# An encoder layer on one core: another split of the first transfers, and four steps moved in a hand-ordered program

## The chip, the cores and the metric

The kernel runs on one core of a Trainium2 chip. The metric is the time of one execution on the device in microseconds (us), lower is better; the figure for the kernel before is the median of three runs. The core has a matrix engine (TensorE, PE in the profile, with its weight loads as a row PEld), three engines for elementwise work (VectorE = DVE, ScalarE = ACT, GpSimd = POOL) and queues that issue transfers between device memory and the on-chip buffers (SP above all, and ACT's own queue at the start; a q behind the engine's name in the trace is its queue's issue).

## The reference

One layer of an encoder is applied to a prompt of 256 tokens and to a sample of 2048 tokens, both of width 1024, with the same weights, in float32:

```python
h = rms_norm(x, g_pre)
q, k, v, z_a, u_f, z_f = split(h @ w_in)          # six groups of 512 columns
y_a = neighbourhood_attention(q, k, v, rpb)       # 8 heads, grid 64 wide, window 8 rows x 16 columns
y_f = fft2(u_f in groups of 64, over tokens and group).real @ w_fourier + b_fourier
mixed = concat([rms_norm(y_a, g_na) * silu(z_a), rms_norm(y_f, g_f) * silu(z_f)])
out = x + rms_norm(mixed @ w_out, g_post)
```

## The kernel before

**Products.** All data are float32. Each operand x is held as a high part xh (x cast to the matrix engine's type) and a low part xl = x - xh, so that a product of two operands is three matmuls into one sum, in the order of `mm3` (lines 163 to 166): high by high (L164), high by the weight's low part (L165), low by the weight's high part (L166); in these calls the first operand is the tokens, the second the weights. A row of the trace names both: L165 reads xh and a weight's low part (vl, or wc), L166 reads xl and a weight's high part. The cast is mostly done by ACT, the subtraction by DVE.

**Order.** The program is ordered by hand: each engine and each queue runs its instructions in the order in which the source issues them, and waits where an operand isn't there yet. Nothing is reordered by a scheduler.

**Stages**, with their places in the profiled execution:

- 0 to 118 us: v and u projections of the first six token tiles (128 tokens each), `p_mm`, and the prompt's z, k and q. Weights arrive in chunks of 128 x 512 (262 KB), are scaled by g_pre and split by `split_w` (ACT L261 writes the high part, DVE L262 the low part, both tiles called wc); token tiles are split by `x_split` (ACT L289, DVE L290).
- 118 to 158 us: `vu(0, ...)`, v and u of two more token tiles by a scheme of seven products of sums (as Strassen's). It has 14 steps of 12 matmuls, one step taking 2.72 us; the steps go j = 0 to 6, twice each. At chosen steps i a table of hooks runs other work ahead of the step's matmuls.
- 158 to 549 us: sixteen passes over pairs of weight blocks, with a second `vu` among them.
- 550 to 593 us: the Fourier stage, that is `z_mm`, `z_turn`, `z_32`, `pq`, then the product with the Fourier matrix.
- 593 to 862 us: attention; 862 to 952 us: output projection; then the last token tile's norm and stores.

**The first transfers (L624 to L627, L639).** x0[0] is one tile of 128 x 776 that holds the eight scales (g_pre, columns 0 to 7), and the first 256 features (two k-slices) of token tiles 0 (columns 8 to 263), 1 (264 to 519) and 2 (520 to 775). ACT's queue issues columns 0 to 519 as one transfer and then tile 2; SP's queue issues the first chunk of v weights (tile rv), then the second, then the rest. While they are on their way PE runs 10 matmuls on ones (L231, tile idle; in the trace each is two passes). Then, per pair of k-slices: first weight chunk, `x_split` of tile 0, copy of the scales to gpre (first pair only, DVE L639), `x_split` of tile 1, second weight chunk, tile 2.

**The hooks of vu(0).** `n_first(j)` makes the operand of product j: a cast of 128 x 2048 on ACT (L434, tile xh) and a subtraction on DVE (L435, tile xl), in full before the step's matmuls are issued. `op_load(j)` (L469) loads the weight sums of product j as two transfers vl, `op_split(j)` splits them (ACT L483 and DVE L484; L479 and L480 for j = 5, which also changes the sign). `rows_load` and `rows_square` load 1 MB of rows (L295, tile xm) and square them on ACT (L300). The finished products are added by DVE (L511, tiles uc, vuo, u4) and stored by SP (L354, vN and uN). `rows_load(6)` and the loads of j = 4 stand on SP's queue behind a store of v.

```python
for x, i in zip(range(3, 7), (0, 3, 5, 7)):
    at(i, n_first, x)
for x in range(4):
    at(2 * x + 1, rows_load, x + 5)
    at(2 * x + 4, rows_square, x + 5)
```

**The Fourier stage.** `z_mm(g)` multiplies into two PSUM tiles ptb (L1028), the same two for each g, and copies them out to zt (L1031, DVE and ACT); `z_turn(g)` transposes zt (L1038), with splits by ACT L1004 and DVE L1005; `z_32` handles the remaining 32 rows (L1019, L1009 to L1012); `pq(m)` is a product of the cosine table with the Fourier weights (L1081), whose result ACT copies to nq (L1087) and splits (ACT L1089, DVE L1090).

```python
z_mm(1); z_turn(0); z_32(0, 1); pq(1)
z_mm(2); z_turn(1); z_mm(3); z_turn(2); z_32(2, 3); z_turn(3); pq(0)
```

**The end.** `last_tile` computes the last output columns in two pieces, of 384 and 128, closes the norm, and for each half of 512 columns runs `residual`: a DVE instruction (L1758) and a store on SP (L1763).

Of the kernel before, what the change touches and what calls it, by code (L numbers as in the profile page):

```python
# [20 lines left out]
KC = 8  # L21
# [141 lines left out]
def mm3(nc, out, lh, ll, rh, rl, first, last):  # L163
    nc.tensor.matmul(out, lh, rh, start=first, stop=False)  # L164
    nc.tensor.matmul(out, lh, rl, start=False, stop=False)  # L165
    nc.tensor.matmul(out, ll, rh, start=False, stop=last)  # L166


def build(tc, A, O):
    nc = tc.nc  # L170
    es = ExitStack()
# [55 lines left out]
    nc.gpsimd.memset(onesq, 1.0)  # L227

    idle = ps.tile([128, 512], F32, tag="c", name="idle", bufs=1)
    for x in range(10):  # L230
        nc.tensor.matmul(idle[:, :128], onesq, onesq, start=True, stop=True)  # L231

    def gt(shape, dtype, name):
# [9 lines left out]
    W = {"v": [], "u": []}  # L243
# [12 lines left out]
    def split_w(m, src, ks=range(2)):  # L256
        for k in ks:
            h, l = chunk(), chunk()
            x = len(W[m])
            g = x0[0][:, x:x + 1] if m == "v" and x < 2 else gpre[:, x:x + 1]  # L260
            nc.scalar.activation(h, src[:, k], AF.Copy, scale=g)  # L261
            nc.vector.scalar_tensor_tensor(out=l, in0=src[:, k], scalar=g, in1=h.bitcast(F32),  # L262
                                           op0=ALU.mult, op1=ALU.subtract)
            W[m].append((h, l))
# [16 lines left out]
    def xload(c):  # L281
        xs[c] = load(BS, A["xs"][c - 3], "xr")

    def x_split(c, ks=slice(0, 8)):
        if c not in xh:
            xh[c] = gt(BS, F32R, "xh"), gt(BS, F32R, "xl")
        h, l = xh[c][0][:, ks], xh[c][1][:, ks]
        src = x_first(c, ks.start // 2) if c < 3 else xs[c][:, ks]
        nc.scalar.copy(h, src)  # L289
        nc.vector.tensor_tensor(out=l, in0=src, in1=h.bitcast(F32), op=ALU.subtract)  # L290


# [37 lines left out]
    def p_mm(m, c, kps, kks=None):  # L330
        if (m, c) not in acc:
            acc[m, c] = ps.tile([128, 512], F32, tag="b", name="mm", bufs=2) if (m, c) == ("u", 2) else mmt(512)
        xh_, xl_ = xh[c]
        for kk in kks or range(2 * kps[0], 2 * kps[-1] + 2):
            mm3(nc, acc[m, c], xh_[:, kk], xl_[:, kk], W[m][kk][0], W[m][kk][1], kk == 0, kk == KC - 1)

    def vu_out(m, c):
        s, b = PL[c]
# [110 lines left out]
    RV, RU = [], []  # L449
# [171 lines left out]
    def x_first(c, kp):  # L621
        return x0[kp][:, 8 * (kp == 0):][:, :768].rearrange("p (c k t) -> p c k t", c=3, t=128)[:, c]

    nc.sync.dma_start(RV[0][:, 0], A["wv"][0][:, 0])  # L624
    nc.scalar.dma_start(x0[0][:, :520], A["x0"])
    nc.scalar.dma_start(x0[0][:, 520:], A["x2"])
    nc.sync.dma_start(RV[0][:, 1], A["wv"][0][:, 1])  # L627
    nc.scalar.preload_act_table_set("natural_log_exp_and_others")
# [1 line left out]
    for kp in range(4):  # L630
        ks = slice(2 * kp, 2 * kp + 2)
        v = part(RV[kp // 2], kp)
        if kp:
            nc.sync.dma_start(v, part(A["wv"][kp // 2], kp))
            nc.sync.dma_start(x0[kp], A["x1"][kp - 1])
        split_w("v", v[:, 0:1], (0,))
        x_split(0, ks)
        if kp == 0:
            nc.vector.tensor_copy(gpre, x0[0][:, :8])  # L639
            x_split(1, ks)  # L640
        split_w("v", v[:, 1:2], (0,))
        if kp:
            x_split(1, ks)
        x_split(2, ks)
# [168 lines left out]
    def at(i, f, *a):  # L813
        hooks.setdefault(i, []).append(call(f, *a))

    for x, i in zip(range(3, 7), (0, 3, 5, 7)):
        at(i, n_first, x)
    for x in range(4):
        at(2 * x + 1, rows_load, x + 5)
# [213 lines left out]
    def z_turn(gq):  # L1033
        for j in range(2):
            p = ps.tile([128, 4, 128], F32, tag="a", name="pab")
            for g in range(4):
                j0 = g % 2 * 256 + j * 128
                nc.tensor.transpose(p[:, g], zt[gq, g // 2][:, j0:j0 + 128], ident)  # L1038
            split_ps(lambda a: a[:, j::2, :1024].rearrange("p m (k q x) -> p q m k x", k=16, q=4)[:, gq]
                     .rearrange("p m k (g l) -> p m k g l", l=4), p.rearrange("p g (m k l) -> p m k g l", m=2, l=4))  # L1040
# [35 lines left out]
    def pq(m):  # L1076
        h, l = PQ[m] = gt([128, 2, 512], F32R, "pqh"), gt([128, 2, 512], F32R, "pql")
        for c in range(2):
            p = ps.tile([128, 512], F32, tag="b", name="ppq", bufs=2)
            for x in range(2):  # L1080
                nc.tensor.matmul(p[64 * x:64 * x + 64], cs2[:, m, :], wf[c][:, x, :], start=True, stop=True)  # L1081
            if m == 0:
                nc.scalar.copy(h[:, c], p)
                nc.vector.tensor_tensor(out=l[:, c], in0=p, in1=f_(h[:, c]), op=ALU.subtract)
                continue
            nq_ = sm.tile([128, 512], F32, name="nq", bufs=2)
            nc.scalar.copy(nq_, p)  # L1087
            nc.gpsimd.dma_start(nw[16 * c:16 * c + 16:4], nq_[::32])
            nc.scalar.activation(h[:, c], p, AF.Copy, scale=dnyq[:, 2:3])  # L1089
            nc.vector.scalar_tensor_tensor(out=l[:, c], in0=p, scalar=dnyq[:, 2:3], in1=f_(h[:, c]),  # L1090
                                           op0=ALU.mult, op1=ALU.subtract)
# [3 lines left out]
    z_mm(1)  # L1095
    z_turn(0)
    z_32(0, 1)
    pq(1)
    z_mm(2)
    z_turn(1)  # L1100
    z_mm(3)
    z_turn(2)
    z_32(2, 3)
# [522 lines left out]
    for k in range(2, len(G) + 1):  # L1626
# [21 lines left out]
        x = k // 2 + 1  # L1648
# [102 lines left out]
        V.tensor_scalar(x, y, s, y, ALU.mult, ALU.mult)  # L1751
        V.tensor_scalar(s, x, 1.5, y, ALU.add, ALU.mult)

    def residual(d, n):
        of, xt, s = d["of"], d["xt"], d["r"][:, 0:1]
        ns = slice(n * 512, n * 512 + 512)
        if "og" in d:
            V.scalar_tensor_tensor(out=xt[:, ns], in0=d["og"][:, ns], scalar=s, in1=xt[:, ns], op0=ALU.mult,  # L1758
                                   op1=ALU.add)
        else:  # L1760
            V.scalar_tensor_tensor(out=of[:, ns], in0=ptb[n], scalar=s, in1=of[:, ns], op0=ALU.mult, op1=ALU.mult)
            nc.gpsimd.tensor_tensor(out=xt[:, ns], in0=of[:, ns], in1=xt[:, ns], op=ALU.add)
        nc.sync.dma_start(O["yo"][d["t"] * 128:d["t"] * 128 + 128, ns], xt[:, ns])  # L1763


    def last_tile(d, b):
        og = d["og"] = gt([128, D], F32, "og")
        nc.gpsimd.tensor_tensor(out=og[:, :512], in0=d["of"][:, :512], in1=gpb[:, :512], op=ALU.mult)
        for q, ns in enumerate((slice(512, 896), slice(896, 1024))):
            p = ps.tile([128, 384], F32, tag="a", name="pl", bufs=3)[:, :ns.stop - ns.start]  # L1770
            for j in range(12):
                c, x = divmod(j, 3)
                nc.tensor.matmul(p, (d["l"] if x == 2 else d["h"])[:, c], WO[x == 1][:, c, ns], start=j == 0,
                                 stop=j == 11)
            if q == 0:
                factor(b)
            residual(b, q)
            evac(d, p, ns, 1 + 2 * q)
        sa = d["sa"]
        V.tensor_scalar(sa[:, 0:1], sa[:, 0:1], sa[:, 1:2], None, ALU.add)  # L1780
        part_sum(sa)
        guess(d, 3)
        V.tensor_tensor(out=og[:, 512:], in0=ptb[1], in1=d["of"][:, 512:], op=ALU.mult)
        factor(d, 3)
        for n in range(2):
            residual(d, n)

    for j, d in enumerate(atiles):
        if j + 3 < 18:
# [46 lines left out]
```

## Time and profile before

| | |
|---|---|
| median of 3 runs | 961.38 us (960.96 to 962.63) |
| the profiled execution, whole | 961.61 us |
| its span in the profile | 959.8 us |
| TensorE clock granted | 0.998 |
| PE busy | 948.7 us, 99% of the span |
| DVE, ACT, POOL busy | 707.3, 496.0, 433.9 us |
| transfers | 269.80 MB, mean 281 GB/s |

Positions in the text are microseconds from the start of the span of that one execution. A row of the timeline gives start, duration (of a group of like instructions, from the first's start to the last's end), engine, line, operation, tiles and shapes, the count, and in brackets the idle time before it with what ended it. Durations of neighbouring instructions overlap a little, since an instruction's end is recorded after the next one has begun. The whole execution is 1.8 us longer than the span; the profiled one is 0.23 us above the median.

### The profile page before, as it was taken

The page shows a single profiled execution, that of the slowest core. Times are in us where ns is not written, and L with a number is a line of the kernel's source. Part 1 is how long each engine was busy: PE and PEld are TensorE (multiplying, and loading weights), DVE is VectorE, ACT ScalarE, POOL GpSimd, SP SyncE. Part 2 cuts the span into 40 slices and gives each one's busy share as a digit, 9 for nine tenths or more (in the row PEclk, how much of TensorE's full clock was granted, in tenths as well). Part 3 has the DMA queues.
Part 4 walks back from the last instruction along what each step waited for, and adds up shares of the span by engine and source line. Part 5 has one row for each costly group of instructions (what it writes and reads, how often), then busy time and mean ns, then how long its engine had stood idle before and what let it go on. Part 6 is the DMA issues. An engine that isn't in the chain of part 4 may idle for free.

```text
span 959.8 us, 16743 instructions
## 1 busy us (share of the span) xinstructions
PE 948.7 (99%) x5625; PEld 789.3 (82%) x5625; DVE 707.3 (74%) x1296; ACT 496.0 (52%) x1069; POOL 433.9 (45%) x411
## 2 busy tenths in 40 slices
PE   9999999999999999999999999999999999999997
PEld 7889987888888888888888779788788888888885
DVE  6758978687886865698887369776665656659997
ACT  6835676423334532233344267677676766644443
POOL 4100002455661302575566045567678686524544
PEclk9999999999999999999999999999999999999999
DMA  9799696558758984499889996698877998989993
GB/s 357 294 382 335 243 360 219 188 204 292 271 214 315 334 320 148 174 347 350 310 289 347 334 331 243 205 261 269 271 231 251 272 293 265 291 277 348 332 339 135
DMA packets 139933, 269.80 MB, mean 281 GB/s; under 512 B 13162, under 2 KB 80192, under 8 KB 136584
## 3 DMA queue, kind: packets, MB, share of 16 engines
q1 hardware_dynamic: 139496, 268.32, 80.4%
q8 instruction: 45, 0.74, 0.3%
q10 hardware_dynamic: 288, 0.40, 0.1%
q14 instruction: 40, 0.33, 0.1%
q0 software_dynamic: 64, 0.02, 0.0%
HBM read 179.00 MB, written 96.81 MB: 287 GB/s over the span
## 4 chain that ended last, share of the span: by engine, by line
PE 94%; DMA 3%; DVE 1%; ACT 1%; issue 0%; SPq 0%; DVEq 0%
PE po L1481 20%; PE mm L165 17%; PE mm L166 17%; PE mm L164 17%; PE pv L1570 6%; PE ptb L1554 6%; PE s L1214 4%; DMA vl<-sD 1%; DMA xm<-xm 1%; PE py L164 1%; PE py L165 1%; PE py L166 1%; PE ptb L1028 1%; DMA x<-x 0%; DVE vl L484 0%; PE pz L165 0%
## 5 line engine op out<-in xcount | busy, mean ns | idle before, releaser
L164 PE MATMUL mm<-xh,wa 128*128 128x512 f32 x448 | 174.4, 389 | 0.0
L165 PE MATMUL mm<-xl,wa 128*128 128x512 f32 x448 | 174.3, 389 | 0.0
L166 PE MATMUL mm<-xh,wa 128*128 128x512 f32 x448 | 174.3, 389 | 0.0
L538 POOL TENSOR_TENSOR ws<-wr 128x512 f32<-128x512 f32 x16 | 23.2, 1447 | 223.9 <-DMA wr<-wz 211.3
L1248 POOL TENSOR_SCALAR w<-w,m 128x465 f32<-128x465 f32 (+9 forms) x136 | 84.9, 637 | 46.0 <-DVE m L1245 35.5
L165 PEld LDWEIGHTS mm<-xl,wa 128*128 128x128 f32 x448 | 84.1, 188 | 17.6
L164 PEld LDWEIGHTS mm<-xh,wa 128*128 128x128 f32 x448 | 84.1, 188 | 17.5
L166 PEld LDWEIGHTS mm<-xh,wa 128*128 128x128 f32 x448 | 84.1, 188 | 17.4
L1481 PE MATMUL po<-wo,yh 128*128 128x512 f32 x272 | 90.5, 413 | 0.0
L553 DVE TENSOR_TENSOR wa<-wr,wa 128x512 fp32r<-128x512 f32 x60 | 73.3, 1230 | 21.7 <-ACT wa L552 21.4
L1481 PE MATMUL po<-w,yh 128*128 128x512 f32 x280 | 86.8, 391 | 0.0
L1241 ACT ACTIVATE w<-w,m 128x465 f32<-128x465 f32 (+9 forms) x136 | 78.3, 579 | 13.6 <-DVE m L1236 13.3
L1236 DVE CUSTOM_DVE_ANT_1 w<-s,tb 128x465 f32<-128x465 f32 (+8 forms) x124 | 61.2, 532 | 10.1 <-PE s L1214 9.4
L165 PE MATMUL mm<-vl,xh 128*128 128x512 f32 x168 | 65.5, 390 | 1.0 <-DVE vl L480 1.0
L166 PE MATMUL mm<-vh,xl 128*128 128x512 f32 x168 | 65.4, 389 | 0.0
L164 PE MATMUL mm<-vh,xh 128*128 128x512 f32 x168 | 65.4, 389 | 0.0
L591 POOL TENSOR_TENSOR mt<-mt,rmask 128x880 f32<-128x880 f32 (+2 forms) x24 | 50.3, 2110 | 31.8 <-DVE mt L587 19.8
L1481 PEld LDWEIGHTS po<-w,yh 128*128 128x128 f32 x280 | 52.2, 188 | 11.0 <-issue 0.4
L1558 DVE COPY pt<-ptb 120x384 f32<-120x384 f32 (+5 forms) x72 | 40.5, 563 | 27.6 <-PE ptb L1554 27.3
L878 DVE TENSOR_TENSOR f<-u,mm 128x512 f32<-128x512 f32 x64 | 43.4, 678 | 22.1 <-PE mm L166 18.4
L1554 PE MATMUL ptb<-ident,w 128*120 128x128 f32 (+8 forms) x422 | 58.9, 276 | 0.0
L552 ACT CAST wa<-wr 128x512 fp32r<-128x512 f32 x60 | 36.5, 618 | 43.1 <-PE mm L166 19.8
(280 smaller groups left out, 2377.0 us busy)
## 6 DMA issues: line engine op xcount, KB each, us to landing
wr<-wz SPq DMA_DIRECT2D x48, 512.0 KB
vl<-sD SPq DMA_DIRECT2D x20, 512.0 KB
xm<-xm SPq DMA_DIRECT2D x9, 1024.0 KB
oD<-ofs SPq DMA_DIRECT2D x18, 512.0 KB
of<-oD SPq DMA_DIRECT2D x18, 512.0 KB
yr<-yD SPq DMA_DIRECT2D x34, 256.0 KB
zD<-f SPq DMA_DIRECT2D x16, 512.0 KB
xD<-nx SPq DMA_DIRECT2D x14, 512.0 KB
```

Of the source, the lines that this page charges most:

```text
L164: nc.tensor.matmul(out, lh, rh, start=first, stop=False)
L165: nc.tensor.matmul(out, lh, rl, start=False, stop=False)
L166: nc.tensor.matmul(out, ll, rh, start=False, stop=last)
L553: nc.vector.tensor_tensor(out=o[:, 1], in0=src, in1=o[:, 0].bitcast(F32), op=ALU.subtract)
L591: nc.gpsimd.tensor_tensor(out=o, in0=i, in1=rmask[:, m0:m0 + n].unsqueeze(2).to_broadcast([128, n, 80]), op=ALU.add)
L878: nc.vector.tensor_tensor(out=dst(f, b), in0=src(uu[u]), in1=src(p), op=op)
L1236: nc.vector.tensor_tensor_reduce(out=rows(g["w"][b][:, h, :n], w), in0=rows(g["s"][2 * b + h][:, :nr * sw(w)], sw(w))[:, :, :w], in1=tv, s ...
L1241: nc.scalar.activation(w, w, AF.Exp, bias=m[:, h:h + 1], scale=-1.0, accum_out=m[:, 2 + h:3 + h])
L1248: nc.gpsimd.tensor_scalar(w, w, m[:, 4 + h:5 + h], 1.0, ALU.mult, ALU.mult)
L1481: nc.tensor.matmul(p, (d["l"] if x == 2 else d["h"])[:, c], w(n, int(x == 1), c), start=j == 0, stop=j == 11)
L1554: nc.tensor.transpose(ptb[h][:nk, j * 128:j * 128 + 128], g["w"][b][:, h, c0:c0 + nk], ident)
L1570: nc.tensor.matmul(p[hs, b], g["v"][:nk, v, hs], g["pt"][b][:nk, h, j * 128:j * 128 + 128], start=j == 0, stop=j == len(ch) - 1)
```

## The change

Five edits, at the start, in the hooks, in the Fourier stage and at the end. Lines of the changed kernel are 6 to 12 higher than those before.

1. Eleven matmuls on ones instead of ten.
2. At the start, ACT's queue issues four transfers instead of two: the scales and tile 0 (264 columns), the last 32 partitions of the first v weight chunk, tile 1 (256 columns), tile 2. SP's first transfer is the other 96 partitions of that chunk. The first split of tile 0 is done wholly by DVE, ahead of the weights' low part, and for the first k-slice of v the three matmuls of a product come in the order high by high, low by high, high by low (`mm3x`).
3. In vu(0) the operands of products 3 to 6 are made at steps 0, 2, 4, 6 instead of 0, 3, 5, 7.
4. pq(1) runs after z_mm(2) and z_turn(1) instead of ahead of them.
5. The last tile's residual is done and stored in pieces of 512, 256 and 256 columns instead of two of 512.

```diff
+def mm3x(nc, out, lh, ll, rh, rl, first, last):
+    nc.tensor.matmul(out, lh, rh, start=first, stop=False)
+    nc.tensor.matmul(out, ll, rh, start=False, stop=False)
+    nc.tensor.matmul(out, lh, rl, start=False, stop=last)
...
-    for x in range(10):
+    for x in range(11):
         nc.tensor.matmul(idle[:, :128], onesq, onesq, start=True, stop=True)
...
-        nc.scalar.copy(h, src)
+        (nc.vector.tensor_copy if vec else nc.scalar.copy)(h, src)
...
-            mm3(nc, acc[m, c], xh_[:, kk], xl_[:, kk], W[m][kk][0], W[m][kk][1], kk == 0, kk == KC - 1)
+            (mm3 if kk or m == "u" else mm3x)(nc, acc[m, c], xh_[:, kk], xl_[:, kk], W[m][kk][0], W[m][kk][1], kk == 0,
+                                              kk == KC - 1)
...
-    nc.sync.dma_start(RV[0][:, 0], A["wv"][0][:, 0])
-    nc.scalar.dma_start(x0[0][:, :520], A["x0"])
+    nc.sync.dma_start(RV[0][:96, 0], A["wv"][0][:96, 0])
+    nc.scalar.dma_start(x0[0][:, :264], A["x0"][:, :264])
+    nc.scalar.dma_start(RV[0][96:, 0], A["wv"][0][96:, 0])
+    nc.scalar.dma_start(x0[0][:, 264:520], A["x0"][:, 264:])
     nc.scalar.dma_start(x0[0][:, 520:], A["x2"])
...
+        if kp == 0:
+            x_split(0, ks, True)
         split_w("v", v[:, 0:1], (0,))
-        x_split(0, ks)
+        if kp:
+            x_split(0, ks)
...
-    for x, i in zip(range(3, 7), (0, 3, 5, 7)):
+    for x, i in zip(range(3, 7), (0, 2, 4, 6)):
         at(i, n_first, x)
...
     z_32(0, 1)
-    pq(1)
     z_mm(2)
     z_turn(1)
+    pq(1)
     z_mm(3)
...
-        for n in range(2):
-            residual(d, n)
+        for ns in (slice(0, 512), slice(512, 768), slice(768, 1024)):
+            residual(d, 0, ns)
```

How the instructions then stand, at the three places where rows change their order (operation, result tile with its buffer number, operands, shape; buffer numbers differ between the kernels).

On VectorE, the first instructions that touch tokens and weights; before:

```order
L262 SCALAR_TENSOR_TENSOR wc_148<-rv_134,x0_138,wc_148 128x512
L290 TENSOR_TENSOR xl_152<-x0_138,xh_151 128x256
L639 COPY gpre_88<-x0_138 128x8
L290 TENSOR_TENSOR xl_157<-x0_138,xh_156 128x256
L262 SCALAR_TENSOR_TENSOR wc_148<-rv_134,x0_138,wc_148 128x512
```

After, on VectorE at the same place:

```order
L295 CAST xh_151<-x0_139 128x256
L296 TENSOR_TENSOR xl_152<-x0_139,xh_151 128x256
L268 SCALAR_TENSOR_TENSOR wc_155<-rv_135,x0_139,wc_155 128x512
L651 COPY gpre_88<-x0_139 128x8
L296 TENSOR_TENSOR xl_160<-x0_139,xh_159 128x256
L268 SCALAR_TENSOR_TENSOR wc_155<-rv_135,x0_139,wc_155 128x512
```

The cast and the subtraction of tile 0 now stand ahead of the first weight chunk's low part, and ACT has one cast fewer behind that chunk's high part.

On VectorE in vu(0), steps 2 to 7; vuo is the sum that SP's queue stores, nt and nx are the sources of n_first; before:

```order
L484 TENSOR_TENSOR vl_1317<-vl_1317,vh_1361 128x1024
L511 TENSOR_TENSOR vuo_1379<-uc_1341,mm_1366 128x512
L435 TENSOR_TENSOR xl_1387<-nt_1037,xh_1386 128x2048
L511 TENSOR_TENSOR vuo_1405<-uc_1358,mm_1392 128x512
L484 TENSOR_TENSOR vl_1320<-vl_1320,vh_1412 128x1024
```

After, on VectorE at the same place:

```order
L491 TENSOR_TENSOR vl_1320<-vl_1320,vh_1363 128x1024
L442 TENSOR_TENSOR xl_1370<-nt_1040,xh_1369 128x2048
L518 TENSOR_TENSOR vuo_1386<-uc_1344,mm_1373 128x512
L518 TENSOR_TENSOR vuo_1408<-uc_1361,mm_1395 128x512
L491 TENSOR_TENSOR vl_1323<-vl_1323,vh_1415 128x1024
```

The subtraction of n_first(4) now stands ahead of the first vuo; those of n_first(5) and n_first(6) move likewise ahead of the first uc and u4 sum.

On ScalarE in vu(0), the casts around the squares of rows (xm); before:

```order
L300 ACTIVATE xm_1390,ssq_133<-xm_1390 128x1024 x2
L434 CAST xh_1481<-nx_809 128x2048
L479 ACTIVATE vh_1502<-vl_1408 128x1024
L479 ACTIVATE vh_1503<-vl_1409 128x1024
L300 ACTIVATE xm_1438,ssq_133<-xm_1438 128x1024 x2
```

After, on ScalarE at the same place:

```order
L441 CAST xh_1467<-nx_812 128x2048
L306 ACTIVATE xm_1393,ssq_134<-xm_1393 128x1024 x2
L486 ACTIVATE vh_1505<-vl_1411 128x1024
L486 ACTIVATE vh_1506<-vl_1412 128x1024
L306 ACTIVATE xm_1441,ssq_134<-xm_1441 128x1024 x2
```

The cast of n_first(6) now stands ahead of the squares of the rows loaded by rows_load(6), and the split of j = 5 follows these squares at once.

On TensorE in the Fourier stage, from z_mm(2) on; ppq is pq(1), pab a z_turn, ptb a z_mm; before:

```order
L1081 MATMUL ppq_4913<-wf_4776,cs2_102 64x512 x2
L1081 MATMUL ppq_4921<-wf_4778,cs2_102 64x512 x2
L1028 MATMUL ptb_4832<-zg_4764,d2_4690 64x256 x4
L1028 MATMUL ptb_4833<-zg_4767,d2_4690 64x256 x4
L1038 MATMUL pab_4941<-ident_83,zt_4874 128x128 x2
L1038 MATMUL pab_4948<-ident_83,zt_4880 128x128 x2
L1028 MATMUL ptb_4832<-zg_4770,d2_4690 64x256 x4
```

After, on TensorE at the same place:

```order
L1040 MATMUL ptb_4835<-zg_4767,d2_4693 64x256 x4
L1040 MATMUL ptb_4836<-zg_4770,d2_4693 64x256 x4
L1050 MATMUL pab_4926<-ident_83,zt_4877 128x128 x2
L1050 MATMUL pab_4933<-ident_83,zt_4883 128x128 x2
L1093 MATMUL ppq_4942<-wf_4779,cs2_102 64x512 x2
L1093 MATMUL ppq_4950<-wf_4781,cs2_102 64x512 x2
L1040 MATMUL ptb_4835<-zg_4773,d2_4693 64x256 x4
```

pq(1) now stands between z_turn(1) and z_mm(3), which writes the same two tiles ptb as z_mm(2). On ACT and DVE the copies and splits of pq(1) move behind those of z_mm(2) and z_turn(1).

More of the change, by code (lines that the diff above doesn't have):

```diff
@@ L282, in xload, with x_split @@
         xs[c] = load(BS, A["xs"][c - 3], "xr")
-    def x_split(c, ks=slice(0, 8)):
+    def x_split(c, ks=slice(0, 8), vec=False):
         if c not in xh:
@@ L1752, in factor, with residual @@
         V.tensor_scalar(s, x, 1.5, y, ALU.add, ALU.mult)
-    def residual(d, n):
+    def residual(d, n, ns=None):
         of, xt, s = d["of"], d["xt"], d["r"][:, 0:1]
-        ns = slice(n * 512, n * 512 + 512)
+        ns = ns or slice(n * 512, n * 512 + 512)
         if "og" in d:
```

## The prediction

> **What bounds the kernel now.** I read the page's busy times first, then what each engine waited for, then the timeline at the waits.
>
> ```profile
> span 959.8 us, 16743 instructions
> PE 948.7 (99%) x5625; PEld 789.3 (82%) x5625; DVE 707.3 (74%) x1296; ACT 496.0 (52%) x1069; POOL 433.9 (45%) x411
> ```
>
> ```profile
> PE mm L164 <- ACT xh L289: 1.2, 1, 1.2
> PE idle L231 <- POOL onesq L227: 1.0, 1, 1.0
> PE mm L165 <- DVE vl L480: 1.0, 1, 1.0
> PE ptb L1028 <- DVE zt L1031: 0.8, 1, 0.8
> ```
>
> TensorE is busy 99% of the span, and these are all its waits. So only three things can gain: the first matmul's wait (1.2 us), the one at L165 in vu(0) (1.0), the one at L1028 in the Fourier stage (0.8), and beside them the tail after PE's last matmul. The change touches these four places; the fourth wait, before the first idle matmul, stays. In between PE runs through, so time saved ahead is kept at the end if what feeds PE moves along. Bounds of the whole: 0.2% of the time (what a measurement can tell from no change) is 1.9 us, and the waits in reach sum to 3.0 us.
>
> **The start.**
>
> ```profile
> 0.73 0.42 ACTq L625 DMA_DIRECT2D x<-x  x1
> 0.99 3.89 PE L231 MATMUL idle<-onesq 128*128 128x128 f32 x20 [0.99 <-POOL onesq L227]
> 1.66 1.28 ACT L628 ACT_TABLE_LOAD   x1 [1.66 <-PEq L1827]
> 5.02 0.72 ACT L261 ACTIVATE wc<-rv,x 128x512 fp32r<-128x512 f32 x1 [1.87 <-DMA x<-x]
> 5.78 0.75 DVE L262 SCALAR_TENSOR_TENSOR wc<-rv,x,wc 128x512 fp32r<-128x512 f32 x1 [4.88 <-ACT wc L261]
> 6.09 0.50 PE L164 MATMUL mm<-wc,xh 128*128 128x512 f32 x1 [1.21 <-ACT xh L289]
> 6.44 0.42 DVE L290 TENSOR_TENSOR xl<-x,xh 128x256 fp32r<-128x256 f32 x1
> 6.78 0.16 DVE L639 COPY gpre<-x 128x8 f32<-128x8 f32 x1
> 7.19 0.74 DVE L262 SCALAR_TENSOR_TENSOR wc<-rv,x,wc 128x512 fp32r<-128x512 f32 x1
> 8.17 0.39 PE L165 MATMUL mm<-wc,xh 128*128 128x512 f32 x1
> ```
>
> ```profile
> 2.00:4.00 2.00, 2.00 (x12) 2.00 (x11) 0.00 (x0) 1.14 (x2) 0.00 (x0) 1.00 0.80 214
> 4.00:6.00 2.00, 0.88 (x8) 0.69 (x7) 0.23 (x1) 0.98 (x3) 0.00 (x0) 1.00 1.07 415
> ```
>
> Everything begins when scales and first weights are there: ACT starts at 5.02, released by the transfer of x. The bytes that must come in for that were 266 KB of x (128 x 520 x 4) and 262 KB of weights, 528 KB; now they are 135 KB, and 262 KB in two pieces, 397 KB. The last column of the two windows is GB/s: at 415 the 131 KB less are 0.32 us, at 214 they are 0.61. If the transfers' fixed part decides and not their bytes, nothing is gained; the weights' second piece is now issued second on ACT's queue, one slot of 0.42 later, which would be a loss of at most that. I take 415, the rate while they land: the data are there at 4.70.
>
> From there: ACT's high part 4.70 to 5.42. DVE meanwhile does tile 0's cast and subtraction; the subtraction takes 0.42, and the cast, for which DVE has no row, lies between a small copy's 0.16 and the subtraction's 0.42, so both are done by 5.54. Then come the weights' low part (5.54), scales and tile 1 and the second low part. Before, the second stood 7.19 - 5.78 = 1.41 us behind the first, of which 0.34 (6.78 - 6.44) was tile 0's subtraction, now done ahead: 5.54 + 1.07 = 6.61, ending 7.35. `mm3x` lets PE begin with the two matmuls that need the weights' high part alone. PE's eighth matmul, the L165 at 8.17, is the first that needs that second low part; it can now run at about 7.43, 0.74 earlier, after which the order of work is as before. With data no earlier (5.02) the same chain gives about 0.45.
>
> Take 0.75; bounds 0 and 1.0. Nothing below 0, since the DVE chain is shorter by 0.34 whenever the data come, against which stands the lost slot of 0.42 at most. What I cost at nothing: the eleventh idle matmul is 2 of now 22 passes, 3.89/20 each, 0.39 in all, ending PE's idle run at 5.27 at most, ahead of the first real matmul at about 5.46. The table load (1.28) moves behind two more issues of 0.42 each, 2.5 to 3.8, covered while ACT waits for data until 4.70; without that cover it would cost what it is late. Tile 2 comes one issue later and is needed only behind twelve matmuls.
>
> By the Trainium skill ("DMA: Bandwidth & Descriptors", section "Rules for kernel authors") two transfers to disjoint groups of partitions go through the same engines and interleave, so that splitting one gains nothing. By that rule the split weights alone would bring 0 from their bytes and this term would be the 0.45; no row of this trace shows a split transfer, and the gain above counts fewer bytes ahead, not a faster path.
>
> **The wait in vu(0).**
>
> ```profile
> 126.66 1.91 ACT L434 CAST xh<-nt 128x2048 fp32r<-128x2048 f32 x1
> 128.00 0.68 DVE L511 TENSOR_TENSOR vuo<-uc,mm 128x512 f32<-128x512 f32 x1
> 128.60 2.29 DVE L435 TENSOR_TENSOR xl<-nt,xh 128x2048 fp32r<-128x2048 f32 x1
> 129.08 0.92 SPq L469 DMA_DIRECT2D vl<-sD  x2
> 130.10 0.38 SPq L295 DMA_DIRECT2D xm<-xm  x1
> 135.40 2.12 ACT L483 CAST vh<-vl 128x1024 fp32r<-128x1024 f32 x2
> 138.98 1.06 ACT L300 ACTIVATE xm<-xm 128x1024 f32<-128x1024 f32 x1 [1.46 <-DMA xm<-xm]
> 140.28 0.39 PE L164 MATMUL mm<-vh,xh 128*128 128x512 f32 x1
> 142.87 2.00 ACT L479 ACTIVATE vh<-vl 128x1024 fp32r<-128x1024 f32 x2
> 145.80 2.35 DVE L480 SCALAR_TENSOR_TENSOR vl<-vl,vh 128x1024 fp32r<-128x1024 f32 x2
> 147.07 0.50 PE L165 MATMUL mm<-vl,xh 128*128 128x512 f32 x1 [0.97 <-DVE vl L480]
> ```
>
> The L165 of j = 5 waits for its weights' low part (145.80 + 1.22). That subtraction stood behind n_first(6)'s subtraction (2.29) and a u sum on DVE, these behind n_first(6)'s cast on ACT, and that behind the squares of rows(6), which waited 1.46 for their transfer. With the cast ahead of these squares, the DVE work is done while ACT squares, and vl follows vh at once.
>
> What the moves cost: n_first(4)'s subtraction now stands ahead of the first vuo on DVE. It can't begin before its cast ends (128.57), so that vuo ends at about 131.5 instead of 128.68. Behind vuo stands its store on SP, and behind that the loads of j = 4 (vl, 129.08) and of rows(6) (130.10): 2.8 later at most. The squares of rows(6) then begin at 138.98 + 2.8 = 141.8 at worst; two squares (2.09 from 138.98 to 141.07) and vh's first half (1.05) and vl's first half (1.2) put L165 at about 146.2 against 147.07: 0.87 saved. Generally L165 comes 4.4 after the landing. j = 4 is tight too: its step begins at 140.28 (less 0.75), its split could begin at 135.40 and can now begin only when vl has landed. At the worst, 138.2, vh's first half and then vl's put its L165 at 140.5, 0.7 later than PE would come for it, which leaves 0.3 of the gain. When the loads were issued before, the queue had work:
>
> ```profile
> 133.00:144.00 11.00, 11.00 (x50) 9.10 (x49) 8.12 (x8) 9.52 (x12) 0.00 (x0) 1.00 1.02 412
> ```
>
> At 412 GB/s for 11 us transfers are the pace of this stretch, so 2.8 later at the issue is less than 2.8 later at the landing only if the engines don't run dry meanwhile; I don't count on that. Take 0.8; bounds -0.5 (rows(6) landing 1.4 later than that worst) and 1.1 (the wait of 0.97 and its slower first matmul).
>
> **The wait in the Fourier stage.**
>
> ```profile
> 555.95 1.94 PE L1081 MATMUL ppq<-wf,cs 128*64 128x512 f32 x8
> 557.72 1.90 PE L1028 MATMUL ptb<-zg,d 128*64 128x256 f32 x16
> 560.03 0.75 DVE L1090 SCALAR_TENSOR_TENSOR pql<-ppq,dnyq,pqh 128x512 fp32r<-128x512 f32 x1 [0.32 <-ACT pqh L1089]
> 560.70 0.68 DVE L1031 COPY zt<-ptb 128x512 f32<-128x512 f32 x1
> 561.43 1.95 PE L1028 MATMUL ptb<-zg,d 128*64 128x256 f32 x16 [0.79 <-DVE zt L1031]
> 564.98 1.09 PE L1038 MATMUL pab<-ident,zt 128*128 128x128 f32 x8
> ```
>
> z_mm(3) writes ptb and waits for DVE's copy of z_mm(2), which stood behind pq(1)'s subtraction on DVE and the copies and splits of pq(1) on ACT. Now z_mm(2) comes 1.77 earlier on PE (557.72 - 555.95), its copies stand ahead of pq(1)'s, and pq(1)'s 1.77 us of matmuls lie between z_turn(1) and z_mm(3): the copy is done by about 559.0, z_mm(3) may start at 561.43 - 0.79 = 560.64. All 0.79 go. Late next would be z_mm(3)'s own copy on DVE behind pq(1)'s two subtractions: these end at about 563.7 (pq's matmuls end at 560.64; copy, high and low part twice, 3.06 as above from 557.72 to 560.78), its copy at 564.4, and z_turn(3), which needs it, comes at 564.19 (564.98 - 0.79): up to 0.24 could come back. Take 0.8; bounds 0.55 and 0.86.
>
> **The tail.**
>
> ```profile
> 951.56 0.61 DVE L1727 SCALAR_TENSOR_TENSOR of<-pl,inva,of 128x384 f32<-128x384 f32 x1
> 952.74 0.34 DVE L1727 SCALAR_TENSOR_TENSOR of<-pl,inva,of 128x128 f32<-128x128 f32 x1
> 955.02 1.41 DVE L1758 SCALAR_TENSOR_TENSOR xt<-og,sr,xt 128x512 f32<-128x512 f32 x2
> ```
>
> ```profile
> 957.50:958.00 0.50, 0.00 (x0) 0.00 (x0) 0.00 (x0) 0.00 (x0) 0.00 (x0) 0.50 0.98 373
> ```
>
> Here only DVE and the last store stand. From 0.34 at 128 columns and 0.61 at 384, 256 columns take about 0.475, two of them 0.95 against 0.71 for 512 in sequence; with the overlap of neighbours 0.13 more. The last store has 128 KB less: 0.35 at 373 GB/s. Take 0.2; bounds -0.13 (the store's fixed part alone decides) and 0.35.
>
> **Sum.** 0.75 + 0.8 + 0.8 + 0.2 = 2.5 off the profiled execution's 961.61, so 959.1; it stood 0.23 above the median, so 958.9 as a median.
>
> **The rivals.** (1) The first transfers land no earlier: the start gives 0.45, the time is 959.2. For it: at 2 to 4 us only 214 GB/s move; against it: 415 until the data are in. The rule of the Trainium skill named above leads to this case, as far as the weights go. (2) The late loads of vu(0) eat its gain, or move the wait to j = 4: 959.6. For it the 2.8 us on SP; against it ACT's idle 1.46 ahead of the squares. (3) What is gained ahead of 550 is swallowed by a stretch in which transfers set the pace (the Fourier stage's loads begin when their buffers come free): only z and tail remain, 1.0, so 960.4. Against it: PE has no other wait in the whole trace. (4) Slower: rows(6) queued on a single SP behind the store come in so late that L165 comes later than before. Its price is landing - 142.67 (147.07 - 4.4); the start's, z's and tail's 1.7 cover it up to a landing at 144.4, and beyond 146.3 the kernel is slower by over 0.2%, above 963.3. Before, this landing was at 138.9; it would need 7.4 us more from 2.8 us at the issue.
>
> **Chances.** My sum 0.50, (1) 0.13, (2) 0.19, (3) 0.10, (4) 0.08. The sum with its terms' spread lies between 957.8 and 960.0 and in five of six cases under 959.46 (0.2% below the median); of (1) two thirds are under it, of (2) a third, of (3) none: 0.42 + 0.09 + 0.06 and rounded up, faster 0.58, same 0.34, slower 0.08. The range for 8 in 10 takes in (1) to (3), 957.8 to 961.0.
>
> **What would show it.** ACT's first weight split at 4.7, PE's first L165 with the second chunk near 7.4 and no wait over 0.3 at the start; no wait on vl at j = 5, the squares of rows(6) behind the cast of n_first(6) at 139 to 142; no wait of z_mm(3) on zt; three stores at the end. The prediction is wrong if PE shows a new wait on vl at j = 4 or 5, on a transfer of the first 30 us, or if the waits are gone and the end is no earlier.

## The result, and the profile after

The change made the kernel slower by 0.2%: 963.83 us median (963.22 to 966.44, 14 runs) against 961.7 us (960.96 to 963.44, 14 runs) for the kernel before, a ratio of 1.0023 with a 95% interval of 1.0016 to 1.0031. The forecast was 958.9, with 957.8 to 961.0 as its range. The profiled execution has a span of 961.9 us against 959.8.

All waits of TensorE in the changed kernel:

```profile
PE mm L165 <- DVE vl L487: 1.8, 1, 1.8
PE idle L237 <- POOL onesq L233: 1.0, 1, 1.0
PE mm L170 <- ACT xh L295: 0.5, 1, 0.5
PE mm L170 <- ACT wc L267: 0.4, 1, 0.4
PE ptb L1566 <- ACT nsb L1542: 0.3, 1, 0.3
```

Of the three waits that should go, the one of z_mm(3) on zt is gone. The one in vu(0) has grown from 1.0 to 1.8. The first matmul's wait has shrunk from 1.2 to 0.4, but only because the idle matmuls now run until 5.95: it starts at 6.31 instead of 6.09. The fourth matmul has a new wait of 0.5, on tile 1's high part.

Where the time went is seen by comparing the places of the same matmuls. Each row holds the matmuls of one line: count, shortest/median/longest duration in ns, and the first and last start in us. First before:

```profile
L166 PE MATMUL mm<-ph,wl x128: 283/283/387, 72.4 to 118.4; 128*128 128x256 f32 x128
L166 PE MATMUL mm<-xh,wa x448: 388/389/397, 158.3 to 549.5; 128*128 128x512 f32 x150
L1214 PE MATMUL s<-kh,qh x140: 272/381/490, 593.6 to 842.7; 64*128 64x360 f32 x32, 64*128 64x480 f32 x32, 64*128 64x288 f32 x16, 64*128 64x384 f32 x16
```

And after:

```profile
L166 PE MATMUL mm<-ph,wl x128: 280/283/386, 73.9 to 119.8; 128*128 128x256 f32 x128
L166 PE MATMUL mm<-xh,wa x448: 388/389/398, 160.6 to 551.7; 128*128 128x512 f32 x150
L1226 PE MATMUL s<-kh,qh x140: 273/381/490, 595.0 to 844.4; 64*128 64x360 f32 x32, 64*128 64x480 f32 x32, 64*128 64x288 f32 x16, 64*128 64x384 f32 x16
```

Ahead of vu(0) PE is 1.4 us late (119.8 - 118.4), behind it 2.3 (160.6 - 158.3), behind the Fourier stage 1.4 again (595.0 - 593.6), at the end of attention 1.7, and the span ends 2.1 later. So the start cost 1.4 and vu(0) 0.9, and the Fourier stage gave back 0.9; 0.3 came from the new wait on nsb at 625 us (attention) and 0.4 from the tail.

The start of the changed kernel:

```profile
1.66 0.45 ACTq L634 DMA_DIRECT2D x<-x  x1
4.62 0.29 DVE L295 CAST xh<-x 128x256 fp32r<-128x256 f32 x1 [3.72 <-DMA x<-x]
5.54 0.72 ACT L267 ACTIVATE wc<-rv,x 128x512 fp32r<-128x512 f32 x1 [1.44 <-DMA rv<-wv]
7.65 0.41 ACT L295 CAST xh<-x 128x256 fp32r<-128x256 f32 x1 [1.39 <-DMA x<-x]
8.11 0.50 PE L170 MATMUL mm<-wc,xh 128*128 128x512 f32 x1 [0.51 <-ACT xh L295]
9.52 0.50 PE L165 MATMUL mm<-wc,xh 128*128 128x512 f32 x1
```

The last 2 us before tile 1 was there, first as a whole (the last number is GB/s), then by queue (q1 is SP's queue, q10 ACT's; packets, MB, and their share of the time of the 16 DMA engines):

```profile
5.60:7.60 2.00, 1.59 (x6) 0.64 (x4) 0.83 (x2) 0.66 (x1) 0.00 (x0) 1.00 1.05 393
```

```profile
q1 hardware_dynamic: 198, 0.59, 76.6%
q10 hardware_dynamic: 210, 0.19, 28.8%
```

The three transfers on ACT's queue release their readers one after the other: tile 0 at 4.62, the 32 rows of weights at 5.54, tile 1 at 7.65, six us after its issue. Before, all of it was there at 5.02. In the 2 us before tile 1's reader started, 786 KB were moved (393 GB/s). SP's queue, whose weights and tokens are wanted later, took 0.59 MB of them; ACT's queue took 0.19 MB, for tile 1 (131 KB) and tile 2 behind it. The two queues moved about as many packets, but SP's were about three times as large. PE's eighth matmul starts at 9.52 instead of 8.17.

And vu(0), the chain that ends at L165 of j = 5:

```profile
133.23 0.92 SPq L476 DMA_DIRECT2D vl<-sD  x2
138.14 1.05 ACT L490 CAST vh<-vl 128x1024 fp32r<-128x1024 f32 x1 [2.25 <-DMA vl<-sD]
140.66 1.90 ACT L441 CAST xh<-nx 128x2048 fp32r<-128x2048 f32 x1
142.47 1.05 ACT L306 ACTIVATE xm<-xm 128x1024 f32<-128x1024 f32 x1
144.68 2.29 DVE L442 TENSOR_TENSOR xl<-nx,xh 128x2048 fp32r<-128x2048 f32 x1 [2.66 <-ACT xm L306]
148.08 2.35 DVE L487 SCALAR_TENSOR_TENSOR vl<-vl,vh 128x1024 fp32r<-128x1024 f32 x2
149.36 0.50 PE L165 MATMUL mm<-vl,xh 128*128 128x512 f32 x1 [1.80 <-DVE vl L487]
```

The loads of j = 4 are issued at 133.23 instead of 129.08, 2.7 later beyond the start's 1.4, and ACT waits for them. The cast of n_first(6) then runs ahead of the squares of rows(6), as the new order has it; but its subtraction (144.68) waits 2.66 us for these squares. Its result takes the buffer that the squared rows leave: xl and xm come from one pool of buffers, handed out in turn. So the subtraction stays behind the squares whatever stands first on ACT, and the vl of j = 5 stands behind the subtraction.

### The profile page after: what moved, and what is told of

Read it like the earlier page. It is cut to its first block, busy times and chain, and to the rows that moved or that the text cites. A ratio compares the mean times of both kernels' runs of the same rounds, so it can differ in the third digit from the quotient of the medians.

```text
span 961.9 us, 16756 instructions
## 1 busy us (share of the span) xinstructions
PE 950.3 (99%) x5627; PEld 790.2 (82%) x5627; DVE 712.6 (74%) x1298; ACT 495.1 (51%) x1068; POOL 434.7 (45%) x411
## 4 chain that ended last, share of the span: by engine, by line
PE 95%; DMA 2%; DVE 1%; issue 0%; SPq 0%; POOL 0%; ACT 0%; ACTq 0%; DVEq 0%; POOLq 0%
PE po L1493 20%; PE mm L165 18%; PE mm L166 18%; PE mm L164 18%; PE pv L1582 5%; PE ptb L1566 5%; PE s L1226 4%; DMA xm<-xm 1%; PE py L164 1%; PE py L165 1%; PE py L166 1%; PE ptb L1040 1%; DMA x<-x 1%; PE pab L1050 0%; PE ppq L1093 0%
## 5 line engine op out<-in xcount | busy, mean ns | idle before, releaser
L165 PE MATMUL mm<-xl,wa 128*128 128x512 f32 x448 | 174.3, 389 | 0.0
L165 PEld LDWEIGHTS mm<-xl,wa 128*128 128x128 f32 x448 | 84.1, 188 | 17.4
L165 PE MATMUL mm<-vl,xh 128*128 128x512 f32 x168 | 65.5, 390 | 1.8 <-DVE vl L487 1.8
```

## The experiments

The first four do one part of the change each.

**The start alone.**

The kernel before with edits 1 and 2 of the change: eleven idle matmuls, the four transfers on ACT's queue, VectorE's split of tile 0 and `mm3x`.

> The kernel before with the edits of the start alone (four transfers on ACT's queue, VectorE's split of tile 0, eleven idle matmuls). Theory (each edit has a price of its own, read by comparing the places of the same matmuls in the two traces): tile 1's transfer lands at about 7.6 us, first v matmuls of tile 1 at 8.1, everything after that 1.4 later than before, up to the last matmul; time +1.4 us. Rival (the start's delay is absorbed by the next place where PE waited, so that the loss in the changed kernel comes from the hooks): PE 1.4 late at 20 us, but the waits of vu(0) and of the Fourier stage shrink by as much, and the time is within 0.5 us of the kernel before.

963.5 us against 961.6, ratio 1.0030 (1.0018 to 1.0041). Tile 1 releases ACT at 7.42; PE is 1.7 late at 120 us (120.1 against 118.4) and 1.6 late at 159.9. The rival falls: vu(0) absorbs 0.1, and the time is 1.9 longer.

**The hooks alone.**

```diff
-    for x, i in zip(range(3, 7), (0, 3, 5, 7)):
+    for x, i in zip(range(3, 7), (0, 2, 4, 6)):
```

> The kernel before with operands 3 to 6 made at steps 0, 2, 4, 6 and nothing else. Theory: the loads of j = 4 are issued 2.7 us later, ACT waits for them near 137, the squares of rows(6) end near 143, and the subtraction of n_first(6), whose result takes the buffer that these squares set free, begins only then; L165 of j = 5 waits 1.8 us instead of 1.0, time +0.9 us. Rival (the prediction's: only the late start of the changed kernel spoils this edit): the wait at L165 goes, time -0.8 us.

962.26 against 961.6, ratio 1.0007 (0.9997 to 1.0016); PE's wait and the subtraction behind the squares:

```profile
PE mm L165 <- DVE vl L480: 1.7, 1, 1.7
143.02 2.29 DVE L435 TENSOR_TENSOR xl<-nx,xh 128x2048 fp32r<-128x2048 f32 x1 [2.67 <-ACT xm L300]
```

PE leaves vu(0) at 159.0 instead of 158.3 with its start unchanged. The prediction's view, that the wait goes, falls in the trace; the times by themselves do not tell +0.7 from nothing.

**The move of pq(1) alone.**

```diff
-    pq(1)
     z_mm(2)
     z_turn(1)
+    pq(1)
```

> The kernel before with pq(1) behind z_turn(1) and nothing else. Theory: PE's wait on zt (0.8 us) is gone, nothing comes in its place, last matmul 0.8 to 0.9 us earlier, time -0.8 us. Rival: what is gained is given back in the attention, where the changed kernel showed a new wait of 0.3 us on the sums of a norm: time -0.5 us.

960.78 against 961.6, ratio 0.9994 (0.9984 to 1.0004), which tells 0.8 neither from nothing nor from more. In the trace there is no wait on zt and none on nsb. All of PE's waits:

```profile
PE idle L231 <- POOL onesq L227: 1.0, 1, 1.0
PE mm L164 <- ACT xh L289: 0.5, 1, 0.5
```

In this execution rows(6) happened to land 1.2 us earlier (squares from 137.77 instead of 138.98), and the wait in vu(0) was gone too, with the program there unchanged. Eight kernels have vu(0)'s order of before and a wait at L165; in each, L165 comes 8.1 us after rows(6) releases ACT (147.07 - 138.98 in the kernel before), so this landing sets the wait. In the seven kernels with that order, this one included, that reach vu(0) within 0.7 us of the kernel before, the release lies between 137.77 and 139.44. A single trace therefore can't tell a few tenths in vu(0) from chance.

**The tail alone.**

```diff
-    def residual(d, n):
+    def residual(d, n, ns=None):
...
-        for n in range(2):
-            residual(d, n)
+        for ns in (slice(0, 512), slice(512, 768), slice(768, 1024)):
+            residual(d, 0, ns)
```

> The kernel before with the last tile's residual in 512, 256 and 256 columns and nothing else. Theory: PE is untouched; the end comes 0.4 us later, since the third store is issued behind the second and a store of half the size ends no sooner after its issue. Rival (the prediction's term): the last store is shorter by 0.35 us, VectorE longer by 0.13, time -0.2 us.

961.18 against 961.6, ratio 0.9998 (0.9989 to 1.0008): not to be told from nothing. From the start of PE's last matmul (952.24) to the end of the span (959.4) it takes 7.2 us, before 7.4 (959.8 - 952.38), in the changed kernel 7.8. The theory of a slower tail falls, and the forecast's 0.2 isn't shown either: with the tail of before the same stretch takes 7.0 to 7.8 in eleven kernels (7.8 in the start-alone kernel, 961.7 - 953.9), with the new tail 7.2 to 7.8 in three.

The next three take the start apart.

**Weights whole.** The start's edits, with the first weight chunk whole on SP's queue.

```diff
-    nc.sync.dma_start(RV[0][:96, 0], A["wv"][0][:96, 0])
+    nc.sync.dma_start(RV[0][:, 0], A["wv"][0][:, 0])
     nc.scalar.dma_start(x0[0][:, :264], A["x0"][:, :264])
-    nc.scalar.dma_start(RV[0][96:, 0], A["wv"][0][96:, 0])
```

> The kernel before with the start's edits, but the first weight chunk whole on SP's queue, so that ACT's queue has three transfers (tile 0 with the scales, tile 1, tile 2). Theory (ACT's queue gets only a small part of the bandwidth while SP's queue holds several transfers, so each transfer put ahead of tile 1 on ACT's queue delays it): without the 32 rows of weights, which took 0.9 us between tile 0's landing and theirs, tile 1 lands at about 6.6 instead of 7.4 to 7.6, the weights at or before 5.4; time +0.4 to +0.8 us. Rival (bytes alone decide, and the order doesn't): tile 1 still lands at about 7.5, time +1.4 us or more.

961.15 against 961.5, ratio 0.9992 (0.9983 to 1.0001).

```profile
4.81 0.72 ACT L267 ACTIVATE wc<-rv,x 128x512 fp32r<-128x512 f32 x1 [1.19 <-DMA x<-x]
5.75 0.41 ACT L295 CAST xh<-x 128x256 fp32r<-128x256 f32 x1 [0.21 <-DMA x<-x]
8.09 0.39 PE L165 MATMUL mm<-wc,xh 128*128 128x512 f32 x1
```

Tile 1 lands at 5.75, earlier than either expected, and the start is no slower than before: the theory's direction holds, its loss of 0.4 to 0.8 doesn't. The first real matmul comes 0.89 after the data (5.70 - 4.81), against 0.77 and 0.78 with the same order of work in three other kernels; no operand is named for it, so the 0.1 is likely that of the 22 idle passes, which end late here (at 6.05, with an overlap).

**Tile 1 on SP's queue**, with the weights still split.

```diff
-    nc.scalar.dma_start(x0[0][:, 264:520], A["x0"][:, 264:])
+    nc.sync.dma_start(x0[0][:, 264:520], A["x0"][:, 264:])
```

> The kernel before with the start's edits, but tile 1's transfer issued second on SP's queue, behind the 96 rows of weights. Theory (queue share): tile 1 lands by about 5.6 and no longer holds anything up; the 32 rows of weights on ACT's queue still land at 5.5 and set the start, the eighth matmul starts at about 8.1, time within 0.3 us of the kernel before. Rival (any transfer of narrow rows lands late, on whichever queue): tile 1 still lands beyond 7, time +1.4 us.

962.29 against 961.5, ratio 1.0009 (1.0000 to 1.0019). ACT is released by the 32 rows of weights at 5.58, tile 1 no longer holds anything up, the eighth matmul starts at 8.40; PE is 0.2 late at 118 us. So tile 1's narrow rows (1 KB each) don't make it late wherever it is issued; what made it late is its place behind others on ACT's queue. Whether wider rows would have helped it there no run shows: beside SP's larger packets that queue got a quarter of the bytes with as many packets.

**The weights split, and nothing else.**

```diff
-    nc.sync.dma_start(RV[0][:, 0], A["wv"][0][:, 0])
+    nc.sync.dma_start(RV[0][:96, 0], A["wv"][0][:96, 0])
     nc.scalar.dma_start(x0[0][:, :520], A["x0"])
+    nc.scalar.dma_start(RV[0][96:, 0], A["wv"][0][96:, 0])
```

> The kernel before with nothing changed but the first weight chunk in two pieces, 96 partitions on SP's queue and 32 on ACT's, second there behind x. Theory (a second transfer on ACT's queue lands about 0.9 us after the first, SP's packets between): scales and tiles at 5.0 or earlier, the last 32 rows of weights at 5.8 to 6.0; the first matmul starts at about 6.9 instead of 6.1, time +0.8 us at 100 us. Rival (the two pieces share the engines and land when one transfer would): first matmul within 0.2 us of 6.1, time unchanged.

962.56 against 961.56, ratio 1.0014 (1.0005 to 1.0023).

```profile
6.02 0.72 ACT L261 ACTIVATE wc<-rv,x 128x512 fp32r<-128x512 f32 x1 [2.40 <-DMA rv<-wv]
7.09 0.79 PE L164 MATMUL mm<-wc,xh 128*128 128x512 f32 x1 [1.47 <-ACT xh L289]
```

32 rows put second on ACT's queue land 1.0 after the 5.02 at which everything was there before (4.78 to 5.07 in seven other kernels with the old transfers). This is worse than the rule weighed in the prediction (the Trainium skill, "DMA: Bandwidth & Descriptors", "Rules for kernel authors": two transfers to disjoint halves of the partitions serialize, so splitting isn't worth it): the trace agrees that nothing is gained, and adds a loss. PE is 2.1 late at 118 us (120.5), since its first matmuls were slow as well (last section), and 1.5 late behind vu(0) (159.8).

**VectorE's split and the matmul order alone**, transfers as before.

```diff
...
+        if kp == 0:
+            x_split(0, ks, True)
         split_w("v", v[:, 0:1], (0,))
-        x_split(0, ks)
+        if kp:
+            x_split(0, ks)
```

> The kernel before, transfers and ten idle matmuls as they were, with VectorE's split of tile 0 ahead of the weights' low part and the other matmul order for the first k-slice alone. Theory: data at 5.0 as before; VectorE does tile 0 while ACT does the weights' high part; the second low part ends at about 7.6, the eighth matmul starts at about 7.7 instead of 8.17; time -0.45 us. Rival (PE itself paces the first matmuls, 0.23 to 0.33 us each, so an earlier operand brings little): the eighth matmul at 8.0 or later, time within 0.2 us.

961.51 against 961.5, ratio 0.9997 (0.9987 to 1.0006): no gain to be seen, though 0.45 lies within the interval. Data are there at 4.79 in this execution, as they are (4.78) in that of the kernel with n_first(4) alone, whose start is that of before: against its 8.00 the eighth matmul at 7.64 is 0.36 early. PE is 0.6 early at 118 us (117.8 against 118.4 before), but behind vu(0) only 0.2:

```profile
PE mm L165 <- DVE vl L487: 1.2, 1, 1.2
L166 PE MATMUL mm<-xh,wa x448: 387/389/398, 158.1 to 549.2; 128*128 128x512 f32 x150
```

In this execution vu(0) takes most of the gain back as a longer wait, because L165 again comes 8.1 behind the release by rows(6) (146.82 - 138.71), and that came only 0.3 earlier. It isn't so in each: with two parts undone (below) PE is 0.7 early at 118 us and 0.9 behind vu(0), with rows(6) at 137.98.

Three kernels take vu(0) apart.

**n_first(6) alone earlier.**

```diff
-    for x, i in zip(range(3, 7), (0, 3, 5, 7)):
+    for x, i in zip(range(3, 7), (0, 3, 5, 6)):
```

> The kernel before with n_first(6) alone a step earlier (0, 3, 5, 6). Theory (the loads of j = 4 are on time again, and n_first(6)'s subtraction waits for the squares of rows(6), whose buffer it takes): squares at 139.4 to 141.5, the subtraction from 141.6, L165 of j = 5 at about 146.4, its wait 0.2 us instead of 1.0; time -0.7 us. Rival (the prediction's, no such buffer): the subtraction runs from 139.4 beside the squares, and L165 of j = 5 doesn't wait at all; time -1.0 us. Second rival: the squares end later than before since the cast stands ahead of them, and the wait at L165 stays at 1.0.

961.16 against 961.5, ratio 0.9996 (0.9986 to 1.0006).

```profile
138.13 1.92 ACT L434 CAST xh<-nx 128x2048 fp32r<-128x2048 f32 x1 [0.46 <-DVE xl L435]
139.96 1.06 ACT L300 ACTIVATE xm<-xm 128x1024 f32<-128x1024 f32 x1
142.17 2.29 DVE L435 TENSOR_TENSOR xl<-nx,xh 128x2048 fp32r<-128x2048 f32 x1 [1.20 <-ACT xm L300]
PE mm L165 <- DVE vl L480: 0.8, 1, 0.8
```

With the loads on time the subtraction still waits for the squares: the buffer is shown without the late loads. The cast waited for a buffer too (0.46), so the gain in this execution is 0.2 and not the 0.7 expected; by the times neither can be told from nothing.

**n_first(4) alone earlier.**

```diff
-    for x, i in zip(range(3, 7), (0, 3, 5, 7)):
+    for x, i in zip(range(3, 7), (0, 2, 5, 7)):
```

> The kernel before with n_first(4) alone a step earlier (0, 2, 5, 7). Theory (late loads and the buffer each hold the chain; this kernel has only the late loads): store of v and the loads behind it 2.7 us later at the issue, rows(6) landing 0.7 to 2 us later, wait at L165 of j = 5 1.7 us or more, time +0.7 us. Rival (the transfers are the pace, so a later issue changes nothing): wait 1.0 as before, time within 0.3 us.

964.55 against 961.56, ratio 1.0031 (1.0022 to 1.0040). In the profiled execution (span 961.2) the loads of j = 4 are issued at 131.56, rows(6) releases ACT at 140.30 instead of 138.98:

```profile
131.56 0.93 SPq L469 DMA_DIRECT2D vl<-sD  x2
140.30 1.06 ACT L300 ACTIVATE xm<-xm 128x1024 f32<-128x1024 f32 x1 [1.47 <-DMA xm<-xm]
PE mm L165 <- DVE vl L480: 2.5, 1, 2.5
```

PE leaves vu(0) at 159.7, 1.4 late. So the later issue does reach the landing: 140.30 lies beyond the 139.44 of the kernels above, and the loss in time is clear of noise. The median lost about as much again as the trace shows. The three executions at 962.94 to 963.03, the profiled one among them, had a granted clock of 0.997; the other seven, at 964.49 to 966.32, had 0.994 to 0.996. By an estimate, 0.002 of PE's 949 busy us is 1.9 us, enough for what the trace leaves open (the seven lie 1.5 to 3.4 above the three). Why the clock was lower isn't shown.

**Rows later**, with pq(1) moved, and VectorE's split and the matmul order as above; all else as before.

```diff
-        at(2 * x + 1, rows_load, x + 5)
-        at(2 * x + 4, rows_square, x + 5)
+        at(2 * x + 3, rows_load, x + 5)
+        at(2 * x + 6, rows_square, x + 5)
```

> The kernel before with pq(1) moved, with VectorE's split of tile 0 and the other matmul order (transfers and ten idle matmuls as before), and with the loads and squares of rows(5) to rows(8) two steps later in vu(0) (loads at steps 3, 5, 7, 9, squares at 6, 8, 10, 12). Theory (the wait at L165 of j = 5 is set by 1 MB loads of rows that run ahead of the weights in a stretch where transfers are the pace, and by the squares whose buffer n_first(6) takes): this wait goes, PE passes vu(0) 1.0 us earlier plus the 0.5 of the start; time -0.5 - 1.0 - 0.8 = -2.3 us. Rival (the pace is the total of the bytes, whatever their order): vl of j = 4 or 5 still comes as late, the wait stays at about 1.2 and the time is -0.8 us, the Fourier stage's part alone.

959.68 (959.20 to 960.66) against 961.56, ratio 0.9980 (0.9971 to 0.9988): faster than both kernels. PE's only wait is the first one, before the idle matmuls:

```profile
PE idle L237 <- POOL onesq L233: 1.0, 1, 1.0
L166 PE MATMUL mm<-xh,wa x448: 388/389/398, 156.8 to 547.9; 128*128 128x512 f32 x150
```

PE leaves vu(0) 1.5 early, 0.4 of it from the start: with one rows load fewer ahead of them, the rows that the chain needs release ACT at 137.44 instead of 138.98. The wait is gone by a narrow margin, as vl of j = 5 is done about when PE comes for it, at 145.60. A release at 137.44 is hardly earlier than the 137.77 that came by chance with the old order, so the trace alone doesn't prove the edit. The times show that the three parts together gain, but not how much of it is the rows'.

**Two parts undone.** The changed kernel with its first weight chunk whole and its hooks as before.

```diff
-    nc.sync.dma_start(RV[0][:96, 0], A["wv"][0][:96, 0])
+    nc.sync.dma_start(RV[0][:, 0], A["wv"][0][:, 0])
     nc.scalar.dma_start(x0[0][:, :264], A["x0"][:, :264])
-    nc.scalar.dma_start(RV[0][96:, 0], A["wv"][0][96:, 0])
...
-    for x, i in zip(range(3, 7), (0, 2, 4, 6)):
+    for x, i in zip(range(3, 7), (0, 3, 5, 7)):
```

> The changed kernel with two parts undone: the first weight chunk whole on SP's queue, and the operands of vu(0) made at steps 0, 3, 5, 7 as before. Theory (these two parts carry the loss): start as in the kernel with whole weights alone, no wait on zt, wait at L165 of j = 5 between 0.7 and 1.3 us; time 960.5, about 1.0 us faster than the kernel before and 3 us faster than the changed kernel. Rival (the loss sits in the eleventh idle matmul, VectorE's split or the third store, which stay): time 962.5 or more.

960.7 against 961.56, ratio 0.9990 (0.9981 to 1.0000); the changed kernel stands at 1.0023. These two parts carry the loss; without them the rest of the change is worth about 0.9 us, barely clear of noise, and about what the move of pq(1) gave alone (960.78). The eleventh idle matmul, VectorE's split and the third store are in it and cost nothing that shows. In the profiled execution the data are there at 4.61 and the eighth matmul starts at 7.45: with the weights whole, the start can do what the prediction said (4.70 and 7.43). The kernel with whole weights above has the same start and came to 4.81 and 8.09, so this holds for some executions only.

## Why the prediction was wrong

**The start (forecast 0.75 faster, bounds 0 to 1.0; 1.4 slower).** The step that failed is "the data are there at 4.70", which counted the bytes needed first and let them have the bandwidth to themselves. They share it with SP's later transfers (0.59 MB on SP's queue against 0.19 on ACT's in the 2 us before tile 1 was there), so a transfer second or third on ACT's queue releases its reader about 0.9 us (weights) and 2 us (tile 1) after the one ahead. The prediction bounded the extra issues at 0.42 of issue time, which was the wrong resource (and with its own 0.34 on the other side even that gave a lower bound of -0.08, not 0); what a further transfer on that queue costs is its landing, 1.0 us with 32 rows alone. It also overlooked that tile 1, now third, is needed by the fourth matmul, and gave only tile 2 a sentence. The saving from fewer bytes is small when the weights are whole: ACT starts at 4.81, and at 4.61 with two parts undone, where kernels with the old transfers had 4.78 to 5.07; 0.2 on the mean, against 0.32 forecast. The compute part (0.45 forecast with data no earlier) measured 0.36 at the eighth matmul, and 0.16 (8.00 - 7.84) in the rows-later kernel, which has the same start. The idle run was mis-sized: 22 passes ended at 5.95, not 5.27, hidden in the changed kernel behind data that came later still; with whole weights it likely cost 0.1.

**vu(0) (forecast 0.8 faster, bounds -0.5 to 1.1; 0.9 slower).** The order on ACT moved as told, and the loads came 2.7 later as told (2.8). What failed is "the DVE work is done while ACT squares": the subtraction needs the buffer of the squared rows. The order shows who stands ahead of whom, not which buffer a result takes, and the row of before (xl at 143.00, released by its cast) hid it, since the cast itself stood behind the squares. The formula "L165 comes 4.4 after the landing" also failed: L165 came 6.9 after the squares began (149.36 - 142.47). And it left out that ACT could be held up by the late vl of j = 4 (2.25 us), which the text had seen for PE, not for ACT. Rival (4), a slower L165, named the late loads and the end, but by a landing of rows(6) beyond 144.4; the queue behind vl of j = 4 and the buffer did it without that.

**The Fourier stage (0.8 forecast).** Right: 0.9 in the changed kernel, no wait on zt, and no wait of z_turn(3) in its place.

**The tail (0.2 forecast).** Not shown: 0.4 slower in the changed kernel's trace, 0.2 faster alone, both within what executions differ by, and the times don't settle it.

**"Time saved ahead is kept at the end"** holds only where what feeds PE moves along. Rival (3) had that right and put it in the wrong place: the stretch that can swallow a gain is vu(0), where L165 follows the landing of rows(6) by 8.1. The compute-only kernel lost most of its gain there (0.6 early before it, 0.2 after), the one with two parts undone didn't (0.7 and 0.9). A loss at the start of 1.7 passed through almost whole (1.6), one of 2.1 as 1.5. How much of a gain lasts on the mean isn't settled by these times.

Open: the wait of 0.3 on nsb at 625 us, which neither the pq(1) kernel nor the two-undone kernel shows, the lower clock in most executions of the kernel with n_first(4) alone, and whether ACT's queue would have fared better with wider rows.

## What to carry to other kernels

Here the third transfer on one queue waited six us while another queue took three quarters of the bytes. So count for each needed transfer what is in flight beside it, and keep what is needed first in few transfers at the head of a queue. When a program moves an instruction ahead of another, look up whose buffer its result takes, since a pool handed out in turn can tie it to the very work that it was moved ahead of. A stage whose wait hangs on transfers can take back time that is gained ahead of it; look whether the transfers move along, and free them first.

## What was not expected of the hardware

The first matmuls after the idle run took 0.50, 0.50, 0.49 us in the kernel before and 0.79 (later ones 0.63) in the kernel with the weights split alone, against 0.39 for the same shape further on, with a granted clock of 1.00 in these stretches. In that kernel the first matmul came 1.0 late (7.09 instead of 6.09), and with this slower pace the eighth came 2.1 late (10.31 instead of 8.17). And the same 20 idle passes took 3.89 us in the execution of before and 4.15 to 4.64 in eight others, so a start varies by some tenths of a microsecond for no reason that the program shows.
